# Block sums for part of the w_up product: seven products for eight in 2 of 8 pairs of k tiles, with banks and buffers laid out anew

## The chip, the core and the metric

The kernel runs on one core of a Trainium2 chip. The core has a matrix engine (TensorE, PE in the profile; its loads of stationary operands are listed apart as PEld), two engines for elementwise work (VectorE, DVE, and ScalarE, ACT), GpSimd (POOL) and SyncE (SP), which here only starts transfers (DMA). On-chip data lie in SBUF, results of matmuls in the eight banks of PSUM, weights in HBM. The metric is the time of one execution in microseconds (us); a profile has a span of its own, from its first to its last instruction.

## What is computed

The kernel is one block of a streaming encoder for 256 tokens of width 2048, in float32: a recurrence and an attention branch, merged by gates, an output projection, and an MLP with squared ReLU. The change concerns the MLP's first product and the buffers from the output projection on:

```python
    merged = gate_a * (y_a @ w_branch_a) + gate_b * (y_b @ w_branch_b)
    return merged @ w_out
...
        h = h + mixer_block(...)
        u = rms_norm(h, norm_mlp_w[l])
        h = h + jnp.square(jax.nn.relu(u @ w_up[l])) @ w_down[l]
    return rms_norm(h, norm_final_w)
```

w_out is 2048 x 2048, w_up 2048 x 8192, w_down 8192 x 2048.

## The kernel before, in words

**Products in three passes.** PE multiplies in a float32 form of reduced precision (float32r). To keep accuracy each operand is split into a high part and the rest: `split` (L86 to L88) casts on ACT (L87, `wh` for weights) and subtracts on DVE (L88, `wl`). A product of one k tile (128 rows of a weight) with one block of 128 tokens (m = 0, 1) and 512 columns is then three matmuls into one PSUM bank: hi·wh (L157), hi·wl (L158), lo·wh (L159).

**Weights.** `weights` (L107 to L144) loads 1 MB at a time (four k tiles of 512 columns) into `raw` (3 buffers), on SP's queue, and splits it in halves of two k tiles (128x1024) into `wh` and `wl` (4 buffers each). These live in the pool `wpool` (L62), which is open from the start to the end of the kernel. The splits stand under `tc.high_priority(offset=2000)`. `gemm` (L149) takes the parts in order of k and runs m = 0 and m = 1 on each, so a part of two k tiles feeds 12 matmuls.

**The order on the engines** is not written out. A scheduler puts each engine's instructions into one queue before the kernel runs, by priority (order of the program, lifted by `high_priority`) among those that by its reckoning are ready; on the chip each engine works its queue in order and waits on semaphores. A tile of a pool takes one of the `bufs` buffers of its tag. Pools lie on a stack: a pool opened after another was closed takes over its ground, and the flag `reuse_waits="tile"` makes a tile there wait for the tiles it covers and not for the whole old pool.

**The boundary before w_out.** The gates' tiles are in `bpool` (L507). For each block of 512 columns `ba` and `bb` are computed and multiplied into the gates (L611), both are added (L615), and `turn` (L600) transposes the sum on PE (`tp_m`, L104) and splits it into `act_m`, the operand of w_out. The last `turn(3)` (L616) stands behind the last bb product. Then `bpool` is closed and `mpool` opened (L620). Its first tiles, `h1`, are eight blocks of the residual, loaded on ACT's queue (L627).

**w_out** (L624 to L640): four blocks of 512 columns; each result is added to the residual (L634), transposed (`tp_h`), weighted (L637) and split into `act_h`, hT[0] to hT[3].

**The MLP** (L653 to L690): four quarters. In each, four blocks of 512 columns of w_up (`acc_up`) go through Relu and Square on ACT (L672, L673) and one step later through `turn` (L658) into `act_u` (transposed, `tp_u`, and split); then four blocks of w_down (`acc_dn`) are added to the residual (L684). PSUM is cut into `ps_acc` (2 buffers of 2 banks, one for each product with both m), `ps_tp` (2 banks for transposes) and `ps_sm` (2 banks). The weights of the final norm, `wf`, are loaded at the start of the MLP (L646) and first used at L690.

Of the kernel before, what the change touches and what calls it, by code (L numbers as in the profile page):

```python
# [8 lines left out]
F32 = mybir.dt.float32  # L9
F32R = mybir.dt.float32r  # L10
# [6 lines left out]
P = 128  # L17
# [33 lines left out]
def tile_hybrid_block(  # L51
# [97 lines left out]
    def gemm(lhs, w, n0, nkt, what, tail=0, kt0=0):  # L149

        acc = [new_acc(f"{what}_{m}")[:, 0, :] for m in range(NM)] if tail else new_acc(what)
        part = (lambda m: acc[m]) if tail else (lambda m: acc[:, m, :])

        def mm(m, kt, wh, wl):
            h = lhs[kt // 4][:, kt % 4, 0, m * P:(m + 1) * P]
            lo = lhs[kt // 4][:, kt % 4, 1, m * P:(m + 1) * P]
            nc.tensor.matmul(part(m), h, wh, start=kt == 0, stop=False)  # L157
            nc.tensor.matmul(part(m), h, wl, start=False, stop=False)  # L158
            nc.tensor.matmul(part(m), lo, wh, start=False, stop=kt == nkt - 1)  # L159
# [440 lines left out]
    def turn(n):  # L600
        mT.append(new_act(f"m{n}"))
        hi, lo = mT[n][:, :, 0, :], mT[n][:, :, 1, :]
        for m in range(NM):
            tp = transpose4(ga[n][m], f"m{n}{m}")
            split(hi[:, :, m * P:(m + 1) * P], lo[:, :, m * P:(m + 1) * P], tp)
# [9 lines left out]
            nc.vector.tensor_tensor(ga[n][m], ga[n][m], gb[n][m], op=ALU.add)  # L615
    turn(3)  # L616
    bpool_cm.__exit__(None, None, None)


    mp = ctx.enter_context(tc.tile_pool(name="mpool", bufs=1, reuse_waits="tile"))  # L620
    h1 = [[None] * NM for _ in range(4)]
    ssq2 = small.tile([P, NM, 4], F32, name="ssq2", tag="ssq2")
    hT = []
    for n in range(4):  # L624
        for m in range(NM):
            t = mp.tile([P, NC], F32, name=f"h1_{n}_{m}", tag="h1", bufs=8)
            nc.scalar.dma_start(t, x[m * P:(m + 1) * P, n * NC:(n + 1) * NC])  # L627
            h1[n][m] = t
        acc = gemm(mT, w_out, n * NC, KD, f"wo{n}")
        hT.append(new_act(f"h{n}"))  # L630
        hi, lo = hT[n][:, :, 0, :], hT[n][:, :, 1, :]
        for m in range(NM):
            t = h1[n][m]
            nc.vector.tensor_tensor(t, acc[:, m, :], t, op=ALU.add)  # L634
            tp = transpose4(t, f"h{n}{m}")
            tmp = mp.tile([P, 4, P], F32, name=f"hw_{n}_{m}", tag="tmp", bufs=4)
            nc.vector.tensor_tensor(tmp, tp, bc(wmlp[:, 4 * n:4 * n + 4], 2, P), op=ALU.mult)  # L637
            split(hi[:, :, m * P:(m + 1) * P], lo[:, :, m * P:(m + 1) * P], tmp)
            junk = mp.tile([P, NC], F32, name=f"hsq_{n}_{m}", tag="tmp", bufs=4)
# [13 lines left out]
    for qd in range(NQ):  # L653
        last = qd == NQ - 1
        uT = []
        pend = []

        def turn():  # L658

            c, rs = pend.pop()  # L660
            uT.append(new_act(f"u{qd}{c}"))
            hi, lo = uT[-1][:, :, 0, :], uT[-1][:, :, 1, :]
            for m in range(NM):
                tp = transpose4(rs[m], f"u{qd}{c}{m}")
                split(hi[:, :, m * P:(m + 1) * P], lo[:, :, m * P:(m + 1) * P], tp)

        for c in range(4):
            acc = gemm(hT, w_up, qd * (FF // NQ) + c * NC, KD, f"up{qd}{c}")
            rs = []
            for m in range(NM):  # L670
                r = mp.tile([P, NC], F32, name=f"r{qd}{c}{m}", tag="tmp", bufs=4)
                nc.scalar.activation(r, acc[:, m, :], AF.Relu, scale=rstd2[:, m:m + 1])  # L672
                nc.scalar.activation(r, r, AF.Square)  # L673
                rs.append(r)
            if pend:
                turn()
            pend.append((c, rs))
        turn()
        for n in range(4):
            end = last and n == 3  # L680
            acc = gemm(uT, w_down, n * NC, KD, f"dn{qd}{n}", tail=8 if end else 0, kt0=qd * KD)
            for m in range(NM):
                t = h1[n][m]
                nc.vector.tensor_tensor(t, acc[m] if end else acc[:, m, :], t, op=ALU.add)  # L684
                if not last:
                    continue
                junk = mp.tile([P, NC], F32, name=f"ysq_{n}_{m}", tag="tmp", bufs=4)
# [60 lines left out]
```

## Time and profile before

| | |
|---|---|
| three runs | 1478.45, 1479.13 (median), 1480.71 us |
| the profiled execution | 1477.8 us, span 1476.0 us, mean granted PE clock 0.995 |
| moved over the span | 270.70 MB, mean 183 GB/s |
| HBM, last gates to w_out | last bb matmul starts at 663.20 us, first w_out matmul at 663.43 us |
| w_up load of 1 MB, issue to landing | 5.0 us (median of 64) |
| transposes of one 128x512 block of u | 4 matmuls; two blocks 0.87 us on the chain |

The page's parts used below: the busy table gives each engine's busy time and share; the chain that ended last names at each step what released the next; a group of instructions shows line, engine, operation, output<-input, shape and count, then busy time and mean of one in ns, then the idle time of the engine before them and what ended most of it. In a timeline a row is start, length, engine, line, operation and tiles; `x2` joins two in one row; what stands in brackets is the idle time before it and its releaser. DMA rows carry the queue's engine with a q.

### The profile page before, as it was taken

The numbers are of one execution on the slowest core, as the hardware profiler recorded it, in microseconds if no ns is written. First come the engines' busy times: TensorE is split into PE (matmuls) and PEld (weight loads), VectorE is DVE, ScalarE is ACT, GpSimd is POOL, SyncE is SP. The second block draws the span as 40 slices with busy tenths as digits, with TensorE's granted clock in tenths as the row PEclk, the third lists the DMA queues.
The fourth block names the chain that finished last, engine by engine and source line by source line (L and its number), as shares of the span: only waits on it lengthen the run. The fifth ranks groups of instructions, "written<-read, shape, count | busy, mean of one in ns | idle before, by whom it ended". The sixth has DMA issues, their size and how long they took to land.

```text
span 1476.0 us, 17274 instructions
## 1 busy us (share of the span) xinstructions
PE 1453.3 (98%) x6854; PEld 1208.9 (82%) x6854; DVE 844.7 (57%) x1115; ACT 707.4 (48%) x890; POOL 46.1 (3%) x93
## 2 busy tenths in 40 slices
PE   7999999999999999999999999999999999999997
PEld 6888888888788888888888888888888888888886
DVE  7897977565644444666554455445544455545554
ACT  5854844464544444444445543445334553345443
POOL 6000001010000000000000000000000000000000
PEclk8999999999999999999999999999999999999999
DMA  6644443545455555557555555555555555555552
GB/s 216 216 170 143 172 171 126 200 123 192 132 180 193 197 200 187 185 194 261 191 180 194 180 194 184 189 199 171 199 197 186 188 177 193 200 197 174 191 186 108
DMA packets 56801, 270.70 MB, mean 183 GB/s; under 512 B 5008, under 2 KB 5648, under 8 KB 39696
## 3 DMA queue, kind: packets, MB, share of 16 engines
q1 hardware_dynamic: 53792, 263.21, 52.3%
q10 hardware_dynamic: 2160, 4.29, 0.9%
q0 software_dynamic: 768, 2.10, 0.8%
q8 instruction: 54, 0.88, 0.2%
q14 instruction: 27, 0.22, 0.0%
HBM read 267.48 MB, written 2.10 MB: 183 GB/s over the span
## 4 chain that ended last, share of the span: by engine, by line
PE 94%; DVE 2%; POOL 2%; issue 1%; ACT 1%; DMA 0%; SPq 0%; POOLq 0%; ACTq 0%; DVEq 0%
PE acc_up L159 8%; PE acc_up L158 8%; PE acc_up L157 8%; PE acc_dn L157 8%; PE acc_dn L159 8%; PE acc_dn L158 8%; PE acc_ak L186 2%; PE acc_wo L158 2%; PE acc_wo L157 2%; PE acc_gb L157 2%; PE acc_wo L159 2%; PE acc_gb L159 2%; PE acc_gb L158 2%; PE acc_ga L158 2%; PE acc_ga L159 2%; PE acc_ga L157 2%
## 5 line engine op out<-in xcount | busy, mean ns | idle before, releaser
L88 DVE TENSOR_TENSOR wl_up<-raw_up,wh_up 128x1024 fp32r<-128x1024 f32 x128 | 156.8, 1225 | 168.4 <-ACT wh_up L87 167.6
L88 DVE TENSOR_TENSOR wl_dn<-raw_dn,wh_dn 128x1024 fp32r<-128x1024 f32 x128 | 156.7, 1224 | 160.7 <-ACT wh_dn L87 160.1
L87 ACT CAST wh_dn<-raw_dn 128x1024 fp32r<-128x1024 f32 x128 | 135.2, 1057 | 200.2 <-PE acc_dn L159 171.8
L87 ACT CAST wh_up<-raw_up 128x1024 fp32r<-128x1024 f32 x128 | 135.3, 1057 | 186.1 <-PE acc_up L159 158.1
L157 PE MATMUL acc_up<-wh_up,act_h 128*128 128x512 f32 x512 | 199.9, 390 | 0.0
L159 PE MATMUL acc_dn<-wh_dn,act_u 128*128 128x512 f32 x512 | 199.5, 390 | 0.0
L157 PE MATMUL acc_dn<-wh_dn,act_u 128*128 128x512 f32 x512 | 199.5, 390 | 0.0
L159 PE MATMUL acc_up<-wh_up,act_h 128*128 128x512 f32 x512 | 199.4, 389 | 0.0
L158 PE MATMUL acc_up<-wl_up,act_h 128*128 128x512 f32 x512 | 199.3, 389 | 0.0
L158 PE MATMUL acc_dn<-wl_dn,act_u 128*128 128x512 f32 x512 | 199.2, 389 | 0.0
L159 PEld LDWEIGHTS acc_dn<-wh_dn,act_u 128*128 128x128 f32 x512 | 96.1, 188 | 19.9
L158 PEld LDWEIGHTS acc_dn<-wl_dn,act_u 128*128 128x128 f32 x512 | 96.1, 188 | 19.8
L159 PEld LDWEIGHTS acc_up<-wh_up,act_h 128*128 128x128 f32 x512 | 96.1, 188 | 19.8
L157 PEld LDWEIGHTS acc_dn<-wh_dn,act_u 128*128 128x128 f32 x512 | 96.2, 188 | 19.7 <-DVE h L684 0.2
L157 PEld LDWEIGHTS acc_up<-wh_up,act_h 128*128 128x128 f32 x512 | 96.1, 188 | 19.7
L158 PEld LDWEIGHTS acc_up<-wl_up,act_h 128*128 128x128 f32 x512 | 96.2, 188 | 19.7
L88 DVE TENSOR_TENSOR wl_gb<-raw_gb,wh_gb 128x1024 fp32r<-128x1024 f32 x32 | 39.2, 1225 | 47.8 <-ACT wh_gb L87 47.8
L88 DVE TENSOR_TENSOR wl_ga<-raw_ga,wh_ga 128x1024 fp32r<-128x1024 f32 x32 | 39.2, 1225 | 43.4 <-ACT wh_ga L87 43.4
L88 DVE TENSOR_TENSOR wl_wo<-raw_wo,wh_wo 128x1024 fp32r<-128x1024 f32 x32 | 39.2, 1224 | 35.6 <-ACT wh_wo L87 35.6
L87 ACT CAST wh_wo<-raw_wo 128x1024 fp32r<-128x1024 f32 x32 | 33.8, 1056 | 49.3 <-PE acc_wo L159 38.3
L87 ACT CAST wh_gb<-raw_gb 128x1024 fp32r<-128x1024 f32 x32 | 33.8, 1057 | 48.6 <-PE acc_gb L159 41.9
L87 ACT CAST wh_ga<-raw_ga 128x1024 fp32r<-128x1024 f32 x32 | 33.8, 1056 | 45.3 <-PE acc_ga L159 38.6
(311 smaller groups left out, 2825.0 us busy)
## 6 DMA issues: line engine op xcount, KB each, us to landing
raw_up<-in_w_up_dram SPq DMA_DIRECT2D x64, 1024.0 KB, 5.0
raw_dn<-in_w_down_dram SPq DMA_DIRECT2D x64, 1024.0 KB, 4.9
raw_ga<-in_w_in_t_dram SPq DMA_DIRECT2D x16, 1024.0 KB, 5.0
raw_gb<-in_w_in_t_dram SPq DMA_DIRECT2D x16, 1024.0 KB, 5.1
raw_wo<-in_w_out_dram SPq DMA_DIRECT2D x16, 1024.0 KB, 5.0
raw_hi<-in_w_in_n_dram SPq DMA_DIRECT2D x8, 1024.0 KB, 5.0
raw_hg<-in_w_in_n_dram SPq DMA_DIRECT2D x8, 1024.0 KB, 5.0
raw_aq<-in_w_in_t_dram SPq DMA_DIRECT2D x8, 1024.0 KB, 4.9
```

The lines of the kernel that those rows point to most:

```text
L87: (copy or nc.scalar.copy)(hi, src)
L88: nc.vector.tensor_tensor(lo, src, hi.bitcast(F32), op=ALU.subtract)
L157: nc.tensor.matmul(part(m), h, wh, start=kt == 0, stop=False)
L158: nc.tensor.matmul(part(m), h, wl, start=False, stop=False)
L159: nc.tensor.matmul(part(m), lo, wh, start=False, stop=kt == nkt - 1)
L186: nc.tensor.matmul(acc[:, cb, :], wh[:, c], r.rearrange("p u t -> p (u t)"), start=kt == 0, stop=kt == nkt - 1)
```

## The change

For a unit of 1024 columns of w_up (two blocks of 512, n = 0, 1) the k tiles are paired: k and k + 8. For the pairs 0 and 1 (k tiles 0, 1, 8, 9) the 2 x 2 block product over (m, n, upper or lower half of k) is formed from seven products of block sums. The sums of activations (`combos`, from hT[0] and hT[2]) are made once; the sums of weights are made in place in the raw tiles, on DVE, in float32, before the split. The seven products go into seven banks; three of these (b11, b12, b21) and an eighth (b22, in the bank that the first product gave back) take the other 12 k tiles in the usual three passes. Five sums out of PSUM (one a copy on ACT) are made behind the products, and four more at the end of the unit give the four result blocks, which then go through Relu and Square as before. The chunks of u that are pending are turned between the products and the rest of the next unit.

To make room, `wpool` and the three PSUM pools are closed after the gates, and new ones opened: `spool` (8 raw buffers of 512 KB, 6 of wh, 6 of wl), `ps_k` (7 banks), `ps_tp2` (1 bank). w_out and w_down use them too, through `gemm2`, which is `gemm` with loads of two k tiles. `wf` moves into a buffer of `apool` and to the last quarter.

```diff
-    wpool = ctx.enter_context(tc.tile_pool(name="wpool", bufs=1))
     apool = ctx.enter_context(tc.tile_pool(name="apool", bufs=8))
     small = ctx.enter_context(tc.tile_pool(name="small", bufs=4))
-    ps_acc = ctx.enter_context(tc.tile_pool(name="ps_acc", bufs=2, space=PSUM))
-    ps_tp = ctx.enter_context(tc.tile_pool(name="ps_tp", bufs=2, space=PSUM))
-    ps_sm = ctx.enter_context(tc.tile_pool(name="ps_sm", bufs=2, space=PSUM))
+    wpool_cm = tc.tile_pool(name="wpool", bufs=1)
+    wpool = wpool_cm.__enter__()
+    ps_cms = [tc.tile_pool(name=n, bufs=2, space=PSUM) for n in ("ps_acc", "ps_tp", "ps_sm")]
+    ps_acc, ps_tp, ps_sm = [cm.__enter__() for cm in ps_cms]
...
+    wpool_cm.__exit__(None, None, None)
+    for cm in ps_cms[::-1]:
+        cm.__exit__(None, None, None)
     mp = ctx.enter_context(tc.tile_pool(name="mpool", bufs=1, reuse_waits="tile"))
+    RT, WB, TB = 8, 6, 9
+    sp = ctx.enter_context(tc.tile_pool(name="spool", bufs=1, reuse_waits="tile"))
+    ps_k = ctx.enter_context(tc.tile_pool(name="ps_k", bufs=7, space=PSUM, reuse_waits="tile"))
+    ps_tp = ctx.enter_context(tc.tile_pool(name="ps_tp2", bufs=1, space=PSUM, reuse_waits="tile"))
...
+    def piece(w, n0, kt, q, what):
+        raw = sp.tile([P, 2 * NC], F32, name=f"raw_{what}", tag="rt", bufs=RT)
+        if w.shape[-1] < NC:
+            nb = NC // T
+            src = w[n0 // T:n0 // T + nb, kt // 8, :, kt % 8:kt % 8 + q, :].rearrange("c p a n -> p c a n")
+            nc.sync.dma_start(raw[:, :q * NC].rearrange("p (c a n) -> p c a n", c=nb, n=T), src)
+        else:
+            nc.sync.dma_start(raw[:, :q * NC].rearrange("p (a n) -> p a n", n=NC), w[n0 // NC, kt // 4, :, kt % 4:kt % 4 + q, :])
...
+    def parts(raw, w, q, what):
+        made = [sp.tile([P, 2 * NC], F32R, name=f"{n}_{what}", tag=n, bufs=WB)[:, :q * NC] for n in ("wh", "wl")]
+        dst, src = made, raw
+        if w.shape[-1] < NC:
+            dst = [t.rearrange("p (a c n) -> p a c n", a=q, n=T) for t in made]
+            src = raw.rearrange("p (c a n) -> p a c n", a=q, n=T)
+        with tc.high_priority(offset=2000):
+            split(dst[0], dst[1], src)
...
+    def mm3(acc, hi, lo, wh, wl, first, last):
+        nc.tensor.matmul(acc, hi, wh, start=first, stop=False)
+        nc.tensor.matmul(acc, hi, wl, start=False, stop=False)
+        nc.tensor.matmul(acc, lo, wh, start=False, stop=last)
+    def lhs_of(lhs, kt, m):
+        return [lhs[kt // 4][:, kt % 4, u, m * P:(m + 1) * P] for u in range(2)]
+    def gemm2(lhs, w, n0, what, kt0=0, tail=0):
+        acc = [bank(f"{what}{m}") for m in range(NM)]
+        held = []
+        def mm(m, k, wh, wl):
+            for a in range(2):
+                mm3(acc[m], *lhs_of(lhs, k + a, m), wh[:, a], wl[:, a], k + a == 0, k + a == KD - 1)
+        for k in range(0, KD, 2):
+            ps = (k, *parts(piece(w, n0, kt0 + k, 2, f"{what}{k}"), w, 2, f"{what}{k}"))
+            if k >= KD - tail:
+                held.append(ps)
+                continue
+            for m in range(NM):
+                mm(m, *ps)
+        for m in range(NM):
+            for ps in held:
+                mm(m, *ps)
+        return acc
...
+    def combos(lhs, n, what):
+        full = []
+        for j in range(2):
+            f = mp.tile([P, n, T], F32, name=f"full_{what}{j}", tag="full", bufs=2)
+            nc.vector.tensor_tensor(f, lhs[2 * j][:, :n, 0, :].bitcast(F32), lhs[2 * j][:, :n, 1, :].bitcast(F32), op=ALU.add)
+            full.append(f)
+        a11, a21 = full[0][:, :, :P], full[0][:, :, P:]
+        a12, a22 = full[1][:, :, :P], full[1][:, :, P:]
+        made = {}
+        s = {i: mp.tile([P, n, P], F32, name=f"s{i}_{what}", tag="tmp", bufs=TB) for i in (5, 2, 4, 7)}
+        nc.vector.tensor_tensor(s[5], a22, a21, op=ALU.subtract)
+        nc.vector.scalar_tensor_tensor(s[2], s[5], -1.0, a11, op0=ALU.mult, op1=ALU.subtract)
+        nc.vector.tensor_tensor(s[4], a12, s[2], op=ALU.add)
+        nc.vector.tensor_tensor(s[7], a11, a21, op=ALU.subtract)
+        for i in (5, 7, 2, 4):
+            t = mp.tile([P, n, 2, P], F32R, name=f"S{i}_{what}", tag=f"S{i}", bufs=1)
+            split(t[:, :, 0, :], t[:, :, 1, :], s[i])
+            made[i] = t
+        return made
+    def gemm_s(lhs, S, w, n0, groups, what, between=None):
+        n1 = n0 + NC
+        b = {i: bank(f"{what}p{i}") for i in ("1", "5", "7", "6", "11", "12", "21")}
+        j = 0
+        nS = sum(groups)
+        for q in groups:
+            B = {}
+            for i, (n, k) in {"22": (n1, 8 + j), "12": (n1, j), "11": (n0, j), "21": (n0, 8 + j)}.items():
+                B[i] = piece(w, n, k, q, f"{what}{i}_{j}")
+            def add(dst, a, c):
+                with tc.high_priority(offset=2000):
+                    nc.vector.tensor_tensor(B[dst], B[a], B[c], op=ALU.add)
+            def product(i, lh, src, n):
+                wh, wl = parts(B[src], w, q, f"{what}{n}_{j}")
+                for a in range(q):
+                    mm3(b[i], *lh(j + a), wh[:, a], wl[:, a], j + a == 0, i in "1567" and j + a == nS - 1)
+            def of(m, jj):
+                return lambda k: lhs_of(lhs, k + 8 * jj, m)
+            def comb(i):
+                return lambda k: [S[i][:, k, u, :] for u in range(2)]
+            product("1", of(0, 0), "11", "p1")
+            product("12", comb(4), "22", "p3")
+            add("22", "12", "22")
+            add("12", "11", "12")
+            product("5", comb(5), "12", "p5")
+            product("7", comb(7), "22", "p7")
+            add("11", "22", "11")
+            product("6", comb(2), "11", "p6")
+            product("11", of(0, 1), "21", "p2")
+            add("21", "11", "21")
+            product("21", of(1, 1), "21", "p4")
+            j += q
+        tmp = lambda n: mp.tile([P, NC], F32, name=f"{n}_{what}", tag="tmp", bufs=TB)
+        s1, X, W, Y, Z = (tmp(n) for n in ("s1", "sx", "sw", "sy", "sz"))
+        nc.scalar.copy(s1, b["1"])
+        nc.vector.tensor_tensor(X, b["6"], s1, op=ALU.add)
+        nc.vector.tensor_tensor(W, b["5"], X, op=ALU.add)
+        nc.vector.tensor_tensor(Y, b["7"], X, op=ALU.add)
+        nc.vector.tensor_tensor(Z, b["7"], W, op=ALU.add)
+        if between:
+            between()
+        b["22"] = bank(f"{what}p8")
+        rest = []
+        for lo in (0, 8):
+            k = lo + nS
+            while k < lo + 8:
+                q = 1 if k % 2 else 2
+                rest.append((k, q))
+                k += q
+        for k, q in rest:
+            end = k + q == KD
+            for n in range(2):
+                wh, wl = parts(piece(w, n0 + n * NC, k, q, f"{what}r{n}_{k}"), w, q, f"{what}r{n}_{k}")
+                for m in range(NM):
+                    i = "12"[m] + "12"[n]
+                    for a in range(q):
+                        mm3(b[i], *lhs_of(lhs, k + a, m), wh[:, a], wl[:, a], i == "22" and (k, a) == (nS, 0), end and a == q - 1)
+        return [(0, 0, b["11"], s1, ALU.add), (1, 0, b["21"], Y, ALU.add), (0, 1, b["12"], W, ALU.subtract), (1, 1, b["22"], Z, ALU.subtract)]
...
-        acc = gemm(mT, w_out, n * NC, KD, f"wo{n}")
+        acc = gemm2(mT, w_out, n * NC, f"wo{n}")
...
-    wf = mp.tile([P, D], F32, name="wf")
-    nc.scalar.dma_start(wf, bass.AP(tensor=norm_final_w.tensor, offset=norm_final_w.offset, ap=[[0, P], [1, D]]))
+    groups = (2,)
+    S = combos(hT, sum(groups), "h")
...
-            c, rs = pend.pop()
+            c, rs = pend.pop(0)
             uT.append(new_act(f"u{qd}{c}"))
             hi, lo = uT[-1][:, :, 0, :], uT[-1][:, :, 1, :]
             for m in range(NM):
                 tp = transpose4(rs[m], f"u{qd}{c}{m}")
                 split(hi[:, :, m * P:(m + 1) * P], lo[:, :, m * P:(m + 1) * P], tp)
-        for c in range(4):
-            acc = gemm(hT, w_up, qd * (FF // NQ) + c * NC, KD, f"up{qd}{c}")
-            rs = []
-            for m in range(NM):
-                r = mp.tile([P, NC], F32, name=f"r{qd}{c}{m}", tag="tmp", bufs=4)
-                nc.scalar.activation(r, acc[:, m, :], AF.Relu, scale=rstd2[:, m:m + 1])
-                nc.scalar.activation(r, r, AF.Square)
-                rs.append(r)
-            if pend:
-                turn()
-            pend.append((c, rs))
-        turn()
+        for c in range(0, 4, 2):
+            rs = {}
+            for m, n, acc, t, op in gemm_s(hT, S, w_up, qd * (FF // NQ) + c * NC, groups, f"up{qd}{c}",
+                                           lambda: [turn() for _ in list(pend)]):
+                with tc.high_priority(offset=2000):
+                    nc.vector.tensor_tensor(t, acc, t, op=op)
+                nc.scalar.activation(t, t, AF.Relu, scale=rstd2[:, m:m + 1])
+                nc.scalar.activation(t, t, AF.Square)
+                rs[m, n] = t
+            for n in range(2):
+                pend.append((c + n, [rs[m, n] for m in range(NM)]))
+        while pend:
+            turn()
+        if last:
+            wf = apool.tile([P, D], F32, name="wf", tag="act")
+            nc.scalar.dma_start(wf, bass.AP(tensor=norm_final_w.tensor, offset=norm_final_w.offset, ap=[[0, P], [1, D]]))
         for n in range(4):
             end = last and n == 3
-            acc = gemm(uT, w_down, n * NC, KD, f"dn{qd}{n}", tail=8 if end else 0, kt0=qd * KD)
+            acc = gemm2(uT, w_down, n * NC, f"dn{qd}{n}", kt0=qd * KD, tail=8 if end else 0)
```

More of the change, by code (lines that the diff above doesn't have):

```diff
@@ new lines, in parts @@
+    def parts(raw, w, q, what):
[6 more added lines that the diff above has]
+            split(dst[0], dst[1], src)
+        return [t.rearrange("p (a n) -> p a n", a=q) for t in made]
@@ new lines, in bank @@
+    def bank(what):
+        return ps_k.tile([P, NC], F32, name=f"acc_{what}", tag="k")
+    def mm3(acc, hi, lo, wh, wl, first, last):
[21 more added lines that the diff above has]
+        return acc
@@ L633, in tile_hybrid_block @@
             t = h1[n][m]
-            nc.vector.tensor_tensor(t, acc[:, m, :], t, op=ALU.add)
+            nc.vector.tensor_tensor(t, acc[m], t, op=ALU.add)
             tp = transpose4(t, f"h{n}{m}")
-            tmp = mp.tile([P, 4, P], F32, name=f"hw_{n}_{m}", tag="tmp", bufs=4)
+            tmp = mp.tile([P, 4, P], F32, name=f"hw_{n}_{m}", tag="tmp", bufs=TB)
             nc.vector.tensor_tensor(tmp, tp, bc(wmlp[:, 4 * n:4 * n + 4], 2, P), op=ALU.mult)
             split(hi[:, :, m * P:(m + 1) * P], lo[:, :, m * P:(m + 1) * P], tmp)
-            junk = mp.tile([P, NC], F32, name=f"hsq_{n}_{m}", tag="tmp", bufs=4)
+            junk = mp.tile([P, NC], F32, name=f"hsq_{n}_{m}", tag="tmp", bufs=TB)
             nc.scalar.activation(junk, t, AF.Square, accum_out=ssq2[:, m, n:n + 1])
@@ L665, in turn @@
                 split(hi[:, :, m * P:(m + 1) * P], lo[:, :, m * P:(m + 1) * P], tp)
-        for c in range(4):
-            acc = gemm(hT, w_up, qd * (FF // NQ) + c * NC, KD, f"up{qd}{c}")
-            rs = []
-            for m in range(NM):
-                r = mp.tile([P, NC], F32, name=f"r{qd}{c}{m}", tag="tmp", bufs=4)
-                nc.scalar.activation(r, acc[:, m, :], AF.Relu, scale=rstd2[:, m:m + 1])
-                nc.scalar.activation(r, r, AF.Square)
-                rs.append(r)
-            if pend:
-                turn()
-            pend.append((c, rs))
-        turn()
+        for c in range(0, 4, 2):
[14 more added lines that the diff above has]
+            nc.scalar.dma_start(wf, bass.AP(tensor=norm_final_w.tensor, offset=norm_final_w.offset, ap=[[0, P], [1, D]]))
         for n in range(4):
             end = last and n == 3
-            acc = gemm(uT, w_down, n * NC, KD, f"dn{qd}{n}", tail=8 if end else 0, kt0=qd * KD)
+            acc = gemm2(uT, w_down, n * NC, f"dn{qd}{n}", kt0=qd * KD, tail=8 if end else 0)
             for m in range(NM):
                 t = h1[n][m]
-                nc.vector.tensor_tensor(t, acc[m] if end else acc[:, m, :], t, op=ALU.add)
+                nc.vector.tensor_tensor(t, acc[m], t, op=ALU.add)
                 if not last:
                     continue
-                junk = mp.tile([P, NC], F32, name=f"ysq_{n}_{m}", tag="tmp", bufs=4)
+                junk = mp.tile([P, NC], F32, name=f"ysq_{n}_{m}", tag="tmp", bufs=TB)
                 nc.scalar.activation(junk, t, AF.Square, accum_out=ssq3[:, m, n:n + 1])
```

1 line of the change is left out of this document (added).

## The prediction

> **What bounds the kernel now.** I read the page's busy table first, then the chain of waits that ended last, then stages of the MLP in the table by windows, then one boundary of stages in the timeline.
>
> ```profile
> span 1476.0 us, 17274 instructions
> PE 1453.3 (98%) x6854; PEld 1208.9 (82%) x6854; DVE 844.7 (57%) x1115; ACT 707.4 (48%) x890; POOL 46.1 (3%) x93
> PE 94%; DVE 2%; POOL 2%; issue 1%; ACT 1%; DMA 0%; SPq 0%; POOLq 0%; ACTq 0%; DVEq 0%
> ```
>
> PE is busy 98% of the span and is 94% of the chain that ended last. The busy number alone would not say so, since matmuls overlap; the chain does. What a matmul is worth is therefore its pitch, start to start, in the stage that changes:
>
> ```profile
> 839.75 0.39 PE L157 MATMUL acc_up<-wh_up,act_h 128*128 128x512 f32 x1
> ...
> 844.28 0.40 PE L159 MATMUL acc_up<-wh_up,act_h 128*128 128x512 f32 x1
> ```
>
> These two are 20 steps apart: 4.53 us / 20 = **0.2265 us** for each 512-column matmul. The 0.39 us of a row is its length and overlaps the next.
>
> ```profile
> L88 DVE TENSOR_TENSOR wl_up<-raw_up,wh_up 128x1024 fp32r<-128x1024 f32 x128 | 156.8, 1225 | 168.4 <-ACT wh_up L87 167.6
> L87 ACT CAST wh_up<-raw_up 128x1024 fp32r<-128x1024 f32 x128 | 135.3, 1057 | 186.1 <-PE acc_up L159 158.1
> L684 DVE TENSOR_TENSOR h<-acc_dn,h 128x512 f32<-128x512 f32 x32 | 20.7, 687 | 11.0 <-PE acc_dn L159 11.0
> ```
>
> The wh cast sat idle for PE to give back a buffer, and wl only for wh. So the split of weights follows PE and has slack. The windows (stretch, its length, then busy us of PE, PEld, DVE, ACT, POOL, then PE clock, DMA share, GB/s) show how much:
>
> ```profile
> 770.00:840.00 70.00, 70.00 (x319) 58.14 (x318) 33.22 (x29) 34.79 (x42) 0.00 (x0) 1.00 0.58 194
> 75.00:95.00 20.00, 19.43 (x93) 16.20 (x92) 18.91 (x48) 11.23 (x19) 0.00 (x0) 1.00 0.56 197
> ```
>
> In w_up (770 to 840) DVE is busy 47% and PE never stops. In the recurrence (75 to 95) DVE is at 95% and PE loses 0.57 us in 20.
>
> **What goes: matmuls.** A unit of 1024 columns (8 of them) had, for the four k tiles 0, 1, 8, 9, 4 tiles x 2 m x 2 n x 3 passes = 48 matmuls; now 7 products x 2 tiles x 3 = 42. Transposes and all other matmuls stay in number. 8 units x 6 x 0.2265 = **-10.9 us**, all on the path. That is the whole gain.
>
> **What is added on DVE and ACT.** Per unit DVE did 16 splits (1.225) and 4 low halves of u (0.686): 22.3 us of some 45.2 (192 x 0.2265 plus 16 transposes). Now: 12 + 7 splits, 4 sums of weights of the same 128x1024 size (taken at the split's 1.225), 8 adds out of PSUM (0.687, row L684) and the 4 low halves: 23.3 + 4.9 + 5.5 + 2.7 = 36.4 us of 43.9, or 83%. ACT goes from 16 x 1.057 + 7.6 (Relu, Square and cast of u, 4 of each) = 24.5 to 28.3 us with 3 casts and one copy. Neither is the bound over a unit. In the products alone DVE needs 11 x 1.225 = 13.5 us and PE only 42 x 0.2265 = 9.5. The cover is the lead: 6 wh/wl pairs, of which PE holds one, and before the products each pair feeds 12 matmuls, 2.72 us, against 1.225 of DVE. Walking the slots back from the first product, five of the seven parts are split before PE gets there, and the last two (slots free at 0 and 1.4 us, each a cast, a subtraction and for one a sum more) are ready at about 2.3 and 5.8 us, wanted at 6.8 and 8.2. So nothing waits, by 2 us. Without that lead it would be 4.0 us a unit, 32 us in all. The price of what still slips is not in this trace; its ends are 0 (row 770 to 840) and 8 x 0.57 = 4.6 us (row 75 to 95, one such 20 us stretch in each unit). I take **+1.0**, near the lower end, because the 0.57 stands in a chain from PE to DVE and back, and here five parts lie between them.
>
> **Banks.** Seven banks hold the products and one the transposes. At a unit's end three are free (p5, p7, p6 after the four PSUM sums), and the others are given back by four adds of 0.687 that start while the last 18 matmuls run (b11 and b21 close 4.1 and 2.7 us before the end). The fourth product, the first that needs one of these, starts 4.1 us into the next unit. Nothing waits. One transpose bank in place of two: a round is 0.45 PE, 0.59 ACT, 0.69 DVE, under 4 us even behind a split; 4 rounds in a unit of 44 us, and PE has other matmuls in its queue. At the turn from w_up to w_down both last chunks of u are now pending, in place of one; w_down's first 8 k tiles (10.9 us) cover two rounds, the next four (5.4 us) the others. All at 0; without the cover, a round is 2 to 4 us, four times.
>
> **Sums of activations** (combos): at most 10 DVE and 4 ACT operations of no more than 0.69 us, once, 6.9 us. They need h0 and h2 alone and lie in the last w_out column block (21.8 us of PE), whose DVE is half idle. 0. The wf load moves off the start of the MLP to the last quarter and has a w_down block (21.8 us) to land in, as against 13.7 us. 0.
>
> **Loads** are 512 KB instead of 1 MB, so twice the issues on SP. Landing takes 2.9 us (256 KB, output) to 5.0 us (1 MB, w_up); I take 4. SP issues nothing else there, 8 buffers lie ahead of the split, and the start of the kernel, where all loads were of 256 KB or less, reached 371 GB/s, against 220 wanted in the products (2.1 MB in 9.5 us):
>
> ```profile
> 8.00:11.00 3.00, 1.79 (x5) 1.21 (x5) 2.49 (x6) 2.93 (x7) 2.43 (x3) 0.50 0.99 371
> ```
>
> So 0; if loads ran one after the other at 4 us against 2.72 of PE, it would be 1.3 us for each of 288.
>
> **What is laid out anew: the boundary from the gates to w_out.** Here I expect the gain to go. Before, the weight pool stays open over it:
>
> ```profile
> 663.20 0.39 PE L159 MATMUL acc_bb<-wh_bb,act_yb 128*128 128x512 f32 x1
> 663.43 0.39 PE L157 MATMUL acc_wo<-wh_wo,act_m 128*128 128x512 f32 x1
> 663.63 1.29 DVE L611 TENSOR_TENSOR gate_gb<-acc_bb,gate_gb 128x512 f32<-128x512 f32 x2 [0.41 <-PE acc_bb L159]
> ...
> 665.96 1.29 DVE L615 TENSOR_TENSOR gate_ga<-gate_ga,gate_gb 128x512 f32<-128x512 f32 x2
> ...
> 666.83 1.20 PE L104 MATMUL tp_m<-ident,gate_ga 128*128 128x128 f32 x8
> ...
> 667.47 1.18 ACT L87 CAST act_m<-tp_m 128x512 fp32r<-128x512 f32 x2
> ...
> 668.07 0.82 ACTq L627 DMA_DIRECT2D h<-in_x_dram  x2
> ```
>
> w_out's matmuls follow the last bb one at once, and they hide the multiply, the add and the transposes of the last merged chunk. The h1 loads show what a new pool costs: they wait for no data, ACT had 1.66 us free every 2.72 us, and still all eight ran behind the last transposes. The order takes nothing of a pool until the pools under it are closed. Now weights, casts and banks of w_out are such tiles too, so in every queue they stand behind the last transposes and their casts. The path becomes, from 663.6: two multiplies and two adds without the split between them, 2.6, to 666.2; the second block's transposes to 667.0; its cast of u is passed, and with it h1 loads, now put ahead of the first weight cast, because its data are not there yet in the order's reckoning: 8 at most, about 6 at 0.41 us (0.82 for two), to 669.5; cast 1.06, subtraction 1.23 to 671.8. One matmul is done before the subtraction ends. From 663.43 to 671.6 less 0.9 of transposes: **+7.3**. Ends: 5 with no h1 load ahead, 10 with all eight at 0.65 us (three took 1.95). The first weights, issued when bb's last matmul frees the ground under them, land at 667.6 and hide behind the h1 loads. Behind the waiting cast stand only further casts; PE has nothing else.
>
> An idle PE also loses clock:
>
> ```profile
> 32.00:34.00 2.00, 2.00 (x8) 1.71 (x7) 2.00 (x2) 0.97 (x2) 1.51 (x2) 0.50 0.00 0
> 34.00:36.00 2.00, 2.00 (x9) 1.73 (x9) 2.00 (x5) 1.11 (x2) 0.00 (x0) 0.70 0.45 98
> 239.00:241.00 2.00, 0.90 (x6) 0.69 (x6) 1.09 (x5) 1.59 (x3) 0.69 (x1) 1.00 0.00 0
> ```
>
> After idle of 1.60 and 2.66 us with one matmul between (26.7 to 31.4 us), the clock stood at 0.50 and 0.70 for 4 us: 1.0 + 0.6 = 1.6 us lost. Around 240, with matmuls in between, nothing was lost. The hole has 4.6 us without any: **+1.5** (0 to 1.6).
>
> **Sum:** -10.9 + 1.0 + 7.3 + 1.5 = -1.1 us against this execution's 1477.8 (its span, 1476.0, and 1.8 around it), 1476.7. That execution lies 1.3 us under the median of the runs shown, so on the median's scale 1479.1 - 1.1 = **1478.0**: no change that can be told (0.2% is 3 us, about what a measurement of this kernel tells from no change).
>
> **Rivals.**
> *The loads and casts cross the boundary.* If w_out's splits are put ahead of the last transposes, PE goes on at 663.4: 1479.1 - 10.9 + 1.0 = 1469.2. For it: the new pools wait tile by tile (the flag reuse_waits), and most of the ground is long dead. Against it: the h1 loads carried the same flag, over dead ground, and were not early.
> *The sums come late.* DVE, at 13.5 us of work against 9.5 in the products, with the four last adds and the PSUM sums in the same queue, delivers a part after PE wants it. It decides once the 2 us of lead are gone; every us a unit is 8 us. At 1.2 us a unit 1487.6; with no lead at all (4.0) 1510. For it: 95% of DVE made PE wait at 75 to 95 us. Against it: the slots walked above.
> *PE stutters.* With a bank for every six matmuls, short waits at each change of product could drop the clock again and again: one drop of 1.6 us in each of 8 units, +13, 1491. [...]
>
> **Chances.** Forecast 0.50 (1473 to 1484.5, by the ends of hole, clock and slips, the low end 0.17 faster, the middle 0.28 within, the high end 0.05 slower); crossing 0.24, faster; late sums 0.20 and stutter 0.06, slower. Faster by over 0.2% 0.41, within 0.28, slower 0.31. The range 1468 to 1490 takes in the crossing case and most of the late sums.
>
> **What would show it.** Right: PE idle from about 663.6 for 7 us but for eight transposes, the windows behind it at a clock under 1; h1 loads ahead of the first wh_wo cast; from w_up on PE at full busy, DVE near 83%. Wrong: first w_out matmul within 1 us of the last bb one (crossing); PE waits on wl_up in the products (late sums); clock under 1 inside w_up (stutter). If PE's pitch in the products is not 0.2265, the first term is wrong.

## The result, and the profile after

The changed kernel takes **1513.37 us** (median of 4 runs, 1513.15 to 1514.03) against 1478.79 for the kernel before on the same chip: a ratio of 1.0234, 95% interval 1.0216 to 1.0252. It is slower by 34.6 us, where 1478.0 was predicted; 1513.37 lies outside the predicted range of 1468 to 1490.

From the page of the kernel after, the span, the busy table and the engines' shares of the chain that ended last:

```profile
span 1511.4 us, 17824 instructions
...
PE 1478.7 (98%) x6806; PEld 1200.8 (79%) x6806; DVE 949.1 (63%) x1245; ACT 733.1 (49%) x926; POOL 46.2 (3%) x93
...
PE 93%; DVE 2%; POOL 1%; issue 1%; ACT 1%; DMA 0%; SPq 0%; ACTq 0%; POOLq 0%; DVEq 0%
```

The 48 matmuls are gone (6854 to 6806), and yet PE is busy for 25 us more and still 98% of the span. So most of the time is not lost in waits. It is in the matmuls themselves, which shows in their pitch (the time from one start to the next), in the timeline of the kernel after, inside one unit of w_up:

```profile
826.91 0.40 PE L655 MATMUL acc_up02p<-wh_up02p,act_h 128*128 128x512 f32 x1
...
827.61 0.39 PE L655 MATMUL acc_up02p<-wh_up02p,act_h 128*128 128x512 f32 x1
...
830.38 0.39 PE L655 MATMUL acc_up02p<-wh_up02p,S_h 128*128 128x512 f32 x1
...
832.42 0.39 PE L655 MATMUL acc_up02p<-wh_up02p,S_h 128*128 128x512 f32 x1
```

The first two rows are three steps apart, 0.70 us / 3 = 0.233; the last two nine, 2.04 / 9 = 0.2267. Same engine, same clock (1.00), weights from the same buffers, three microseconds apart: what differs in kind is the stationary operand (which PEld loads), activations (`act_h`) here, their block sums (`S_h`) there; the moving operand is a weight in both. Over the whole trace every kind of 512-column matmul with weights moving and activations stationary has a mean pitch of 233.3 to 233.5 ns, also where the code did not change, against 226.7 to 227.8 before (neighbours of the same kind; steps over 245 ns, which hold a wait, a transpose or a slow clock, left out).

The waits of PE in the kernel after (total, times, longest):

```profile
PE acc_up00p L655 <- ACT S_h L87: 4.8, 1, 4.8
...
PE acc_wo L655 <- ACT wh_wo L87: 2.8, 1, 2.8
PE tp_m L104 <- DVE gate_ga L615: 2.1, 1, 2.1
```

Two places, then: the boundary from the gates to w_out (second and third row), which was predicted, and the start of w_up (first row), which was not. The boundary in the timeline:

```profile
674.18 0.40 PE L159 MATMUL acc_bb<-wh_bb,act_yb 128*128 128x512 f32 x1
674.38 15.41 SPq L637 DMA_DIRECT2D raw_wo<-in_w_out_dram  x13
...
676.65 1.23 PE L104 MATMUL tp_m<-ident,gate_ga 128*128 128x128 f32 x8 [2.07 <-DVE gate_ga L615]
677.32 1.19 ACT L87 CAST act_m<-tp_m 128x512 fp32r<-128x512 f32 x2 [12.75 <-PE tp_m L104]
677.92 1.42 ACTq L777 DMA_DIRECT2D h<-in_x_dram  x3
...
679.62 1.04 ACT L87 CAST wh_wo<-raw_wo 128x1024 fp32r<-128x1024 f32 x1 [1.12 <-issue]
...
680.72 1.22 PE L655 MATMUL acc_wo<-wh_wo,act_m 128*128 128x512 f32 x2 [2.84 <-ACT wh_wo L87]
```

After the last bb matmul PE has only the last transposes until 680.72; the first weight cast stands behind the transposes' casts and three h1 loads. The start of w_up:

```profile
758.86 0.69 DVE L688 TENSOR_TENSOR full_h<-act_h 128x512 f32<-128x512 f32 x1
...
779.86 0.68 DVE L787 TENSOR_TENSOR hw<-tp_h,vt 128x512 f32<-128x512 f32 x1
780.46 0.41 DVE L694 TENSOR_TENSOR s_h<-full_h,full_h 128x256 f32<-128x256 f32 x1
```

The activations that the sums need are ready at 759.55, but the first sum runs at 780.46, right behind the last `hw` of w_out's last block. The windows (length, then busy us of PE, PEld, DVE, ACT, POOL, clock, DMA share, GB/s) of the two holes, of two whole units of w_up, and of a stretch of both w_up and w_down:

```profile
678.00:686.00 8.00, 5.24 (x14) 3.77 (x15) 5.86 (x6) 5.45 (x6) 0.00 (x0) 0.58 0.98 362
...
783.00:788.00 5.00, 4.83 (x13) 3.29 (x13) 2.20 (x6) 1.07 (x3) 0.00 (x0) 0.60 0.32 109
...
963.00:1051.00 88.00, 88.00 (x389) 71.19 (x388) 63.07 (x64) 47.35 (x54) 0.00 (x0) 1.00 0.61 207
1000.00:1150.00 150.00, 150.00 (x662) 120.92 (x661) 93.04 (x92) 74.00 (x85) 0.00 (x0) 1.00 0.54 179
```

Behind each hole the clock is low (0.58 and 0.60). Later PE never stops; DVE is busy 72% of the two units of w_up (63.07 of 88 us), where the prediction had 83%, and 62% of the longer stretch.

### The profile page after: what moved, and what is told of

The parts are those of the page before. It is cut to its first block, busy times and chain, and to the rows that moved or that the text cites. A ratio compares the mean times of both kernels' runs of the same rounds, so it can differ in the third digit from the quotient of the medians.

```text
span 1511.4 us, 17824 instructions
## 1 busy us (share of the span) xinstructions
PE 1478.7 (98%) x6806; PEld 1200.8 (79%) x6806; DVE 949.1 (63%) x1245; ACT 733.1 (49%) x926; POOL 46.2 (3%) x93
## 4 chain that ended last, share of the span: by engine, by line
PE 93%; DVE 2%; POOL 1%; issue 1%; ACT 1%; DMA 0%; SPq 0%; ACTq 0%; POOLq 0%; DVEq 0%
PE acc_dn L657 8%; PE acc_dn L655 8%; PE acc_dn L656 8%; PE acc_wo L655 2%; PE acc_wo L656 2%; PE acc_wo L657 2%; PE acc_gb L159 2%; PE acc_gb L158 2%; PE acc_gb L157 2%; PE acc_ak L186 2%; PE acc_ga L159 2%; PE acc_ga L158 2%; PE acc_ga L157 2%; PE acc_aq L186 2%; PE acc_hq L186 2%; PE acc_hf L186 1%
## 5 line engine op out<-in xcount | busy, mean ns | idle before, releaser
L655 PE MATMUL acc_dn<-wh_dn,act_u 128*128 128x512 f32 x512 | 203.1, 397 | 0.0
L657 PE MATMUL acc_dn<-wh_dn,act_u 128*128 128x512 f32 x512 | 202.8, 396 | 0.0
L656 PE MATMUL acc_dn<-wl_dn,act_u 128*128 128x512 f32 x512 | 202.8, 396 | 0.0
L655 PE MATMUL acc_wo<-wh_wo,act_m 128*128 128x512 f32 x128 | 51.4, 403 | 2.8 <-ACT wh_wo L87 2.8
L186 PE MATMUL acc_hf<-act_x,wh_hf 128*128 128x512 f32 x128 | 49.5, 419 | 3.0 <-DVE act_x L88 3.0
L656 PE MATMUL acc_wo<-wl_wo,act_m 128*128 128x512 f32 x128 | 51.3, 401 | 0.0
L657 PE MATMUL acc_wo<-wh_wo,act_m 128*128 128x512 f32 x128 | 51.2, 400 | 0.0
L159 PE MATMUL acc_ga<-wh_ga,act_x 128*128 128x512 f32 x128 | 51.2, 400 | 0.0
L157 PE MATMUL acc_ga<-wh_ga,act_x 128*128 128x512 f32 x128 | 51.1, 399 | 0.0
L158 PE MATMUL acc_ga<-wl_ga,act_x 128*128 128x512 f32 x128 | 51.0, 398 | 0.0
L157 PE MATMUL acc_gb<-wh_gb,act_x 128*128 128x512 f32 x128 | 50.6, 396 | 0.0
```

What stands on the lines that cost most here:

```text
L186: nc.tensor.matmul(acc[:, cb, :], wh[:, c], r.rearrange("p u t -> p (u t)"), start=kt == 0, stop=kt == nkt - 1)
L655: nc.tensor.matmul(acc, hi, wh, start=first, stop=False)
L656: nc.tensor.matmul(acc, hi, wl, start=False, stop=False)
L657: nc.tensor.matmul(acc, lo, wh, start=False, stop=last)
```

## The experiments

**The two theories on the pitch.** The change opens `apool` (activations) and `small` ahead of `wpool`, so all addresses move. Before, `apool` began right above `wpool`; in the built program the first wh buffer and the first activation buffer are 32,768 bytes apart. After, `small` lies between them, and its 6,080 bytes are no multiple of 256; the distance is 65,536 (activations) + 6,080 + 24,576 (raw) = 96,192 bytes. All tiles of both kinds begin at multiples of 512 bytes from these. *Theory A*: the distance between the moving operand (weights) and the stationary one, modulo some small power of two, sets the pitch (first put as modulo 128). *Theory B*: it is the place of the activations, low in SBUF. Each kernel below ran once, but for e6 (10 runs) and e7 (12). Of 23 runs of the kernel before beside the last ones, 21 took 1477.48 to 1480.06 us and two 1486.96 and 1487.88, so a single time with a difference of under 10 us is no proof; the pitch, which the trace gives thousands of times, is.

**e1_order**: the kernel before, with nothing but the pools' order changed.

```diff
-    wpool = ctx.enter_context(tc.tile_pool(name="wpool", bufs=1))
     apool = ctx.enter_context(tc.tile_pool(name="apool", bufs=8))
     small = ctx.enter_context(tc.tile_pool(name="small", bufs=4))
+    wpool = ctx.enter_context(tc.tile_pool(name="wpool", bufs=1))
```

> The kernel before with one thing changed: apool and small are opened ahead of wpool, so that wpool lies behind them in SBUF, as in the changed kernel. Instructions and their order stay. In the changed kernel a 512-column matmul with a stationary operand from apool takes 233.5 ns start to start where it took 226.7, from the first gemm on, also in stages whose code did not change. Theory A (addresses: what counts is how the stationary and the moving operand lie to each other modulo 128 bytes): the pitch is 233.5 in all of ga, gb, wo, up and dn, 4990 such matmuls x 6.8 ns = +34 us, 1511. Theory B (addresses: a stationary operand low in SBUF, under some 91 KB, is read slower): the same, 1511. Rival (the pitch comes with the new instruction stream, the new PSUM pools or the smaller loads): 226.7 and 1478.

Measured 1511.24 against 1478.37 for the kernel before on the same chip: **+32.9 us** from the order of three lines, with the same instructions. Its timeline, 18 steps apart:

```profile
670.82 0.40 PE L159 MATMUL acc_bb<-wh_bb,act_yb 128*128 128x512 f32 x1
...
675.01 0.40 PE L159 MATMUL acc_bb<-wh_bb,act_yb 128*128 128x512 f32 x1
```

4.19 / 18 = 0.2328. 32.9 us over the 5184 matmuls of this kind is 6.3 ns each.

**e2_pad64**: the changed kernel with a dead tile of 64 bytes at the end of `small`, so that the distance becomes 96,256, a multiple of 1024.

```diff
+    pad = small.tile([P, 16], F32, name="pad", tag="pad", bufs=1)
+    nc.gpsimd.memset(pad, 0.0)
```

> The changed kernel with 64 bytes of padding at the end of small, so that wpool, mpool and spool all lie 64 bytes higher and apool stays. Moving weights were at 96 modulo 128 and stationary activations at 32; now both are at 32. Theory A: the pitch falls to 226.7 with act as the stationary operand, 4940 matmuls x 6.7 = 33 us less, 1480 for the profiled run; the two holes (before w_out and in the first products) stay. Theory B (low addresses are slow): apool has not moved, 233.5, 1511. If it is 64 and not 128 bytes that count, also 1511.

Measured 1485.83: **64 bytes take away 27.5 us**, and the pitch is 227 ns everywhere, here over 18 steps, 4.08 / 18 = 0.2267:

```profile
659.22 0.39 PE L161 MATMUL acc_bb<-wh_bb,act_yb 128*128 128x512 f32 x1
...
663.30 0.39 PE L161 MATMUL acc_bb<-wh_bb,act_yb 128*128 128x512 f32 x1
```

Both holes stay, in its waits of PE:

```profile
PE acc_up00p L657 <- ACT S_h L89: 4.8, 1, 4.8
...
PE acc_wo L657 <- ACT wh_wo L89: 3.0, 1, 3.0
```

**e3_right_off**: the changed kernel with the activations at the high end of SBUF and, as in e2, the tile of 64 bytes in `small`; the distance is off the multiple (-107,840).

```diff
-    apool = ctx.enter_context(tc.tile_pool(name="apool", bufs=8))
+    apool = ctx.enter_context(tc.tile_pool(name="apool", bufs=8, side="right"))
```

> The changed kernel with apool at the upper end of SBUF (163808 to 229344) and the weights below it, with 64 bytes of padding so that weights stand at 32 and activations at 96 modulo 128. Theory A: unequal modulo 128, so act as stationary operand keeps 233.5, 1511. The stationary sums S lie with the weights and keep 226.7. Theory B: apool is high now, 226.7, 1480, and S, now low (under 79 KB), goes to 233.5.

1513.23, pitch 233 with `act` and 227 with `S_h`. Theory B falls: high activations are as slow (233.3 ns, as in after).

**e4_align**: the kernel before with 96 bytes added in `const`, so that weights and activations move together.

> The kernel before with 96 bytes of padding at the end of const: weights and activations both start on multiples of 128 (before both at 32). Theory A, if only the difference counts: 226.7 and 1478. [...] Theory B: 226.7 and 1478.

1478.42, 227 ns: moving the pair by 96 bytes, to a multiple of 256, changes nothing. With before and e2, whose pairs lie elsewhere again, only the distance is left.

**g32, g128, g512, g256, g480**: the kernel before with a dead pool of so many bytes between `wpool` and `apool`; nothing else moves against each other. For 512:

```diff
     wpool = ctx.enter_context(tc.tile_pool(name="wpool", bufs=1))
+    padp = ctx.enter_context(tc.tile_pool(name="padp", bufs=1))
+    pad = padp.tile([P, 128], F32, name="pad")
+    nc.gpsimd.memset(pad, 0.0)
     apool = ctx.enter_context(tc.tile_pool(name="apool", bufs=8))
```

> The kernel before with an unused tile of 32 bytes between wpool and apool: activations stand 32 bytes off the weights modulo 128 instead of 0 (measured so far: 0 gives 226.7 ns for a 512-column matmul, 64 gives 233.5). If any difference modulo 128 costs the full step: 233.5 ns and 1511. If the step grows with the distance: some 230 ns, 1495. If it is a clash of two places exactly 64 bytes apart: 226.7, 1478.

> The same with 128 bytes between. Theory A (the difference modulo 128): 226.7 ns, 1478. So far every fast case had a difference that is a multiple of 1024; if a longer period than 128 counts, the pitch is 233.5 here, 1511.

> The same with 512 bytes between: 226.7 and 1478 under theory A and under any period up to 512; 233.5 and 1511 if the period is 1024 or more.

> The kernel before with 256 bytes put between its weight pool and its activation pool (moving operand minus stationary operand: 256 modulo 512, where 480, 448, 384 and 192 were slow and 0 was fast). If the period is 256 bytes: pitch 227 ns, about 1478. If the period is 512 bytes: pitch about 233, about 1506 to 1511.

> The same with 480 bytes (moving minus stationary: 32 modulo 512, the one side of the full multiple that no run has tried). If only the full multiple is fast: pitch 232 to 234 ns, 1506 to 1511. If a moving operand a little ahead of the multiple is as good as on it: 227 ns, about 1478.

| kernel | weights' address minus activations', modulo 256 | mean pitch, ns | us |
|---|---|---|---|
| before, e2, e4 | 0 | 226.8, 227.0, 226.8 | 1478.4, 1485.8, 1478.4 |
| g256 | 0 | 226.8 | 1477.11 |
| g512 | 0 | 226.8 | 1477.76 |
| g480 | 32 | 233.3 | 1509.58 |
| g128 | 128 | 232.5 | 1506.31 |
| after, e1, e3 | 192 | 233.3, 233.3, 233.3 | 1513.4, 1511.2, 1513.2 |
| g32 | 224 | 233.3 | 1508.18 |

(The kernel before took 1478.37, 1478.47 and 1478.7 beside these.) The table has means, because medians mislead here: in the slow kernels neighbouring steps often alternate, in the timeline of after from 826.91 on 236, 231, 235, 231 ns, so the median of a kind is 231 or 235 though its mean is 233.3. g128 refuted theory A as first put: the period is not 128. g256 settles it at 256, as far as these distances go. In the timelines of g256 (first two rows) and g480, 18 steps each:

```profile
658.33 0.39 PE L162 MATMUL acc_bb<-wh_bb,act_yb 128*128 128x512 f32 x1
...
662.41 0.39 PE L162 MATMUL acc_bb<-wh_bb,act_yb 128*128 128x512 f32 x1
```

```profile
669.30 0.40 PE L162 MATMUL acc_bb<-wh_bb,act_yb 128*128 128x512 f32 x1
...
673.50 0.40 PE L162 MATMUL acc_bb<-wh_bb,act_yb 128*128 128x512 f32 x1
```

4.08 / 18 = 0.2267 and 4.20 / 18 = 0.2333. Of the remainders tried none lies in the middle: 32 bytes off costs as much as 192 or 224 (233.3 ns), and 128 nearly so (232.5). In the changed kernel `S_h` lies 40,960 bytes from the first new wh buffer, a multiple of 256, which fits the pace that its matmuls kept (0.2267).

**e5_sums**: e2 with the sums of activations called behind block 2 of w_out (they need hT[0] and hT[2] alone) in place of behind block 3.

```diff
+        if n == 2:
+            groups = (2,)
+            S = combos(hT, sum(groups), "h")
     ssum2 = small.tile([P, NM], F32, name="ssum2", tag="ssum")
...
-    groups = (2,)
-    S = combos(hT, sum(groups), "h")
```

> The changed kernel with the 64 bytes of padding, and combos called after the third column block of w_out instead of after the fourth. In the changed kernel the sums s_h were ready to be made at 760 us (full_h1 was done at 759.5, DVE had 1.57 us free twice) and ran at 780.5, behind the residual adds of the last block; PE waited 4.8 us for S_h and ran at half clock after it. Theory: they share the tag tmp, whose buffers are given out in the order of the program, so they had to follow hw and hsq of the last block. Then here S_h is ready before the products begin, the wait and the clock loss go, about 7 us less than with padding alone (1485.8): 1479. Rival: the products wait for their weights all the same (the sums of weights come late): PE waits on wh or wl instead and the time stays above 1483.

1475.76: 10.1 us less than e2, one run each; the last stage of the table further down has 8.5 of it, and e5's waits of PE have no `S_h` any more. Its timeline:

```profile
745.18 0.69 DVE L690 TENSOR_TENSOR full_h<-act_h 128x512 f32<-128x512 f32 x1
747.20 0.42 DVE L696 TENSOR_TENSOR s_h<-full_h,full_h 128x256 f32<-128x256 f32 x1
...
750.24 1.09 DVE L90 TENSOR_TENSOR S_h<-s_h,S_h 128x256 fp32r<-128x256 f32 x3
```

```profile
762.98 0.65 PE L106 MATMUL tp_h<-ident,h 128*128 128x128 f32 x4
763.39 0.48 PE L657 MATMUL acc_up00p<-wh_up00p,S_h 128*128 128x512 f32 x1
```

The sums are done 12 us before PE wants them, and the first product with `S_h` starts without a wait (the second fence), so the late sums were the cause of that wait. In the changed kernel the tiles `s_h` share the tag `tmp` with `hw` and `hsq`, whose buffers are given out in the order of the program, so those of block 3 went first; that it is the tag and not the place in the queue alone was not separated.

**e6_h1**: e5 with the h1 loads issued on SP, behind the block's weights, in place of ACT.

```diff
+        acc = gemm2(mT, w_out, n * NC, f"wo{n}")
         for m in range(NM):
...
-            nc.scalar.dma_start(t, x[m * P:(m + 1) * P, n * NC:(n + 1) * NC])
+            nc.sync.dma_start(t, x[m * P:(m + 1) * P, n * NC:(n + 1) * NC])
...
-        acc = gemm2(mT, w_out, n * NC, f"wo{n}")
```

> The kernel with the pad and the early sums (1475.8), its h1 loads issued on SP behind the weight loads of their block in place of ACT. If the h1 issues on ACT delay the first weight cast of w_out, as the prediction had it: the cast comes up to 1.1 us earlier (its idle put down to issue) and the time is 1474.5 to 1475.2. If the landing of the first w_out weights (issued when the last branch matmul ends) is the limit: the cast stays about 5.4 us behind that matmul and the time is 1475.8.

1477.5 (10 runs), against 1478.7 for the kernel before: 0.9987, 0.9975 to 1.0. The cast now follows the transposes' casts at once, in the waits of PE:

```profile
PE acc_wo L657 <- ACT wh_wo L89: 1.6, 1, 1.6
```

1.6 in place of 2.8 in e5, as the first reading had it; but the gain does not reach the end, and neither expected time came. (e5's one run, 1475.76, lies inside e6's range of 1475.61 to 1478.57: in the traces e6 loses its 3 us against e5 in the first stage, which no edit touches.) From the last bb to the last w_out matmul it is 98.42 us, in e5 98.70. The hole, from the last bb to the first w_out matmul, shrinks by 1.4 us; but behind the shorter one 12 matmuls run in steps of 0.43 us or more, behind the longer one 7, and these five steps at about 0.2 us each take back 1.0.

**e7_raw**: e6 with three pools in place of `spool`, in the order wl, raw, wh, so that the first raw buffers lie on ground dead since the attention.

> The kernel of e6 with the pools of the MLP's weights in the order wl, raw, wh, so that the first two raw buffers lie on ground that has been dead since the attention and their loads need not wait for the last branch matmul. If the landing is the limit of the first cast: the cast directly follows the last cast of the merged activations, about 1 us earlier than in e6, and 1 us less in all. If the order (casts behind the last transposes) is the limit: the same as e6. In both the pitch stays at 227 ns, since all distances stay multiples of 512 bytes.

1477.08 (12 runs): 0.9987, 0.9971 to 1.0003, the same wait of 1.6. Its loads did not go out earlier (the first at 666.27, 2.4 us behind the last bb matmul), and the cast directly followed the last cast of the merged activations, as it did in e6 already; so the landing is not the limit of the first cast, the order is. That the new pools would let the loads go out early was not borne out, and why they waited was not looked into. A version that puts w_out's casts ahead of the last transposes was not run.

## Why the prediction was wrong

From the starts of matmuls in the timelines:

| stage, us | before | after | e2 | e5 | e6 |
|---|---|---|---|---|---|
| to the last bb matmul | 663.20 | 674.18 | 663.30 | 662.11 | 665.17 |
| from there to the last w_out one | 91.21 | 100.86 | 99.06 | 98.70 | 98.42 |
| first w_up to last w_down | 712.34 | 727.13 | 712.50 | 703.95 | 703.99 |

(The first stage moves by 1.5 us either way from one execution to the next.) By the prediction's terms:

| term | predicted | measured | from |
|---|---|---|---|
| matmuls that go | -10.9 | -10.9 | by count: 48 fewer, 0.227 each |
| slips in the products | +1.0 (0 to 4.6) | +2.5 | e5 against before, last stage: -8.4 + 10.9 |
| hole before w_out and its clock | +7.3 + 1.5 | +5.5 + 2.0 | e5 against before, middle stage |
| sums of activations | 0 | +8.5 | e2 against e5, last stage |
| pitch of all other matmuls | 0, not a term | +27.5 | after against e2 |
| sum | -1.1 | +35.1 | 34.6 by the medians |

**The step that failed** is in "What goes: matmuls". Its pitch was right for the products (0.2267), and the sentence "Transposes and all other matmuls stay in number" was taken to mean that they stay in time. The part "What is laid out anew" priced the new order of the pools for what it does to waits, at one boundary. It did not ask what new addresses do to 4944 matmuls that nobody touched; nothing in the trace of before shows an address, and one pitch of 0.2265 was all it had. The runs showed a cost of 6.5 ns for each of them at the distance that the new order makes (remainder 192 modulo 256), and of 5.7 (128) to 6.5 (32 and 224) at the other remainders tried; 4944 x 6.5 = 32 us would be the estimate from the pitch alone, and the times differ by 27.5 because e2 gives some back (fourteen slow steps behind the wait for `S_h` against eight, and 0.68 us in place of 0.61 for each group of transposes). The test that it named ("If PE's pitch in the products is not 0.2265, the first term is wrong") looked in the wrong place: the products with `S_h` have 0.2267, and everything around them has 0.233.

**A second step failed**, "Sums of activations ... 0". The work was sized rightly (6.9 us at most, and DVE half idle), its inputs too. What failed is "lie in the last w_out column block": they are in the program behind that block and came behind it in DVE's queue. The 21.8 us of cover were there and not used. The wait of 4.8 us and the slow steps behind it (in e2 fourteen of 0.42 us or more, 14 x 0.19 = 2.7 over the 0.227 of the others) are 7.5 of the 8.5 us; the rest was not assigned.

**The hole before w_out** was right in place and mechanism, and its size came out near by luck: 7.5 for 8.8. In e5 the first w_out matmul starts 6.67 us behind the last bb one, against 0.23 before; less the 0.9 of transposes that is 5.5 us of hole, where 7.3 stood. The slow steps behind it cost 2.0, where 1.5 stood with 1.6 as its end; seven steps at the granted clock of 0.50 (e5, 668 to 672) alone would be 1.4. Of h1 loads, three stood ahead of the cast where six were assumed; e6 shows that their place is worth 1.2 us at the cast and some 0.3 in the end.

**The slips** measured +2.5, within their range, but are not what the prediction priced. PE's waits in e5 name no split of w_up at all. In the last stage the time beyond 226.7 ns a matmul is 16.2 us before and 18.7 in e5, and all of it lies at the transposes of u and h and in the fourteen steps behind each group of them. One row of before and one of e5:

```profile
799.20 1.04 PE L104 MATMUL tp_u<-ident,r 128*128 128x128 f32 x8
```

```profile
813.81 0.60 PE L106 MATMUL tp_u<-ident,s_up 128*128 128x128 f32 x4
```

Before, the 136 transposes came in 16 groups of eight and two of four, in e5 in 34 groups of four, each at 0.55 us on average: twice as many interruptions of the matmuls. So the late splits cost nothing, as the walk of the slots said, and the part "Banks", which put one transpose bank in place of two at 0, is where the 2.5 us belong. That it is the single bank and not the new place of the transposes in the program was not separated.

With the two failed terms taken away the stages of e5 give -10.9 + 2.5 + 7.5 = -0.9 for -1.1 predicted, and e6 and e7 lie 1.2 and 1.6 us under the kernel before. Neither can be told from no change (their intervals reach to 1.0 and 1.0003), and that the sum fits is in part luck: the slips are 1.5 over and the hole with its clock 1.3 under.

**The rivals.** The crossing did not come: the first w_out matmul started 6.5 us behind the last bb one. The late sums of weights did not: DVE had 72% of two units and PE was never idle in them. The stutter, the author's estimate, did not: with seven banks in turn the granted clock stands at 1.00 in that window (963 to 1051 us), as it does from 788 to 1496 us.

## What to carry to other kernels

A change of pool order is a change of addresses, and on this kernel, which PE bounds, it cost more (27.5 us, after against e2) than the arithmetic it made room for gained (10.9): compare the mean pitch of matmuls, over many steps, in *unchanged* stages before reading any wait. For matmuls as here, with weights moving and activations stationary, the pitch was 226.8 to 227.0 ns in every run with a multiple of 256 bytes between the two kinds of buffers and 232.5 to 233.3 at the four other remainders tried, so keep such a multiple: dead pools of 32, 128 and 480 bytes between them cost 28 to 31 us here (g32, g128, g480), and a dead tile of 64 bytes took 27.5 away (e2). And work whose inputs are ready early is not done early for that: the sums could have run at 759.55 and ran at 780.46, and in e5, called a block sooner, at 747.20.

## What was not expected of the hardware

The pitch of a 512-column float32r matmul that takes weights as moving and activations as stationary operand is 226.8 to 227.0 ns on average in the runs whose addresses differ by a multiple of 256 bytes (before, e2, e4, g256, g512), 233.3 ns at the remainders 32 (g480), 192 (after, e1, e3) and 224 (g32), and 232.5 at 128 (g128). Other remainders were not tried, and moving the pair together had no effect in e4 (226.8). The step is not there at once: in the changed kernel the first three to six matmuls with `S_h` of each unit but the first still run at 228 to 236 ns (231, 231, 236, 228, 233, 230 from 828.31 on) before the rest settle at 226 to 227. Steps of that size also follow transposes in e5 (225 to 236 ns behind 814.48), so they are no sign of the addresses alone. Why it is so stays open: the weight loads of w_down have the same mean in both traces (188 ns). For the matmuls with the roles exchanged (the recurrence's `hf`, activations moving) it is not settled: their median on `wh` was 233 ns before and 229 in g32, where the matmuls with weights moving were slower.
